# Down projection: five right-hand operands split during the gates and parked in DRAM, products reordered, ends on DVE

## The chip, the cores and the metric

One core of one Trainium2 chip runs the kernel. The metric is the device time of one execution in microseconds (us). Three executions before the change took 2123.8, 2124.66 and 2126.33; the median is 2124.66.

The engines that the text names: PE (matmul), ACT (ScalarE), DVE (VectorE), POOL (GpSimd), SP (the queue that issues most DMAs).

## The reference, cut to what matters

One block of a diffusion backbone on 1024 latent tokens with `D_MODEL` 1024, `D_FF` 2816, batch 1, all in float32, and a context prefix of 256 tokens. The two places of the change:

```python
merged = jax.nn.sigmoid(gate_a) * (y_a @ w_a) + jax.nn.sigmoid(gate_b) * (y_b @ w_b)
return merged @ w_o
...
a, v = jnp.split(h @ w_up, 2, axis=-1)
a = dwconv_grid(a, conv_w, conv_b) if on_grid else dwconv_seq(a, conv_w, conv_b)
return (jax.nn.gelu(a) * v) @ w_down
```

`w_down` is 2816 x 1024. The result of the block goes through a residual addition and a final RMSNorm to the output.

## The kernel before

**Products.** A float32 operand is split into a high part (rounded to fp32r, by an ACT cast) and a low part (the rest, by a subtraction). A product is three matmuls, high x high, high x low and low x high (`mm3`, L97 to L99). One matmul of 512 columns follows the one before in 0.23 us.

**Weights.** All weights come in units of 128 x 1024 elements (512 KB). A unit is loaded by SP into one of three slots `wraw` (`W_RAW`), cast by ACT into one of three slots `whi` and subtracted into one of three slots `wlo` (`W_SPL`), on POOL in the gates (L79). A slot is free again when its last reader is done: for `wraw` the subtraction, for `whi` and `wlo` the last matmul of the unit. Each engine and the queue of SP work strictly in the order that was written down at build time; an instruction that waits holds all behind it.

**Stages named here.** Gate A (about 967 to 1145 us): for each block m of 8, a unit of `w_in` (G0 to G7) and a unit of `w_branch_a` (B0 to B7), 48 matmuls each. Gate B (about 1145 to 1330): the same with `w_in` (G'0 to G'7) and `w_branch_b` (B'0 to B'7), in the order G'0, G'1, B'0, G'2, B'1 and so on; its inputs `ybl` and `ybh` are eight tiles that are loaded, cast and split at the border, when B7 has let go of the buffers. Beside both gates runs `mod_step`: a load `maw` of 512 KB into one buffer and a multiply-add on DVE. Then the output projection, the up projection with the convolution, and from 1871 us the down projection.

**Down projection.** It is done as Strassen's scheme with seven products on quarters (A: hidden values, B: `w_down`), each over six units `u` of two 128-row pieces (the last of one), 24 matmuls to a unit, 132 to a product. Four of the seven right-hand operands are differences of quarters of `w_down`; `sums_down(m)` makes them in gate A, for m below 6: four loads, four DVE subtractions (L113), four stores `t_d`. In the down projection every right-hand unit is loaded raw, cast by ACT (L1238) and subtracted by DVE (L1239). The left-hand operand of a unit is made by DVE (sums, L1213; low part, L1199) and ACT (cast, L1198). Behind the units stand the `ends`: additions of products out of PSUM (DVE), multiplication by the gate `g2b` and the residual addition (`gmul` L1316, `gadd` L1317, on POOL), the sum of squares (ACT), the factor of the norm, and the store. `reload(1)` loads the second half of the hidden values, 22 loads in one block behind the last weight load of the first product.

Of the kernel before, what the change touches and what calls it, by code (L numbers as in the profile page):

```python
# [8 lines left out]
F32 = mybir.dt.float32  # L9
# [26 lines left out]
def kernel(  # L36
# [29 lines left out]
    t_d = {(i, u): dram.tile([P, 1024], F32, name=f"t{i}_d{u}") for i in (1, 2, 3, 4) for u in range(NU)}  # L66
# [44 lines left out]
    def sums_down(u):  # L111
        n = unit_len(u) * 512
        sub = lambda o, a, b: nc.vector.tensor_tensor(out=o, in0=a, in1=b, op=ALU.subtract)  # L113
        keep = lambda i, t: nc.sync.dma_start(out=t_d[i, u][:, 0:n], in_=t)
        b12, b11 = raw_down(u, 0, 512), raw_down(u, 0, 0)
        sub(b11, b12, b11)
        keep(1, b11)
        b22 = raw_down(u, 1, 512)
        sub(b12, b22, b12)
        keep(3, b12)  # L120
        sub(b22, b22, b11)
        keep(2, b22)
        b21 = raw_down(u, 1, 0)
        sub(b21, b21, b22)
        keep(4, b21)
# [734 lines left out]

    for m in range(KC):
# [317 lines left out]
    reload(0)  # L1179
# [54 lines left out]
    def parts_b(raw, u):  # L1234
        n = unit_len(u) * 512
        hi = wp.tile([P, 1024], F32R, tag="whi", name="whi", bufs=W_SPL)[:, 0:n]
        lo = wp.tile([P, 1024], F32R, tag="wlo", name="wlo", bufs=W_SPL)[:, 0:n]
        nc.scalar.copy(out=hi, in_=raw)  # L1238
        nc.vector.tensor_tensor(out=lo, in0=raw, in1=f32(hi), op=ALU.subtract)  # L1239
        return v2(hi, u), v2(lo, u)  # L1240

    def quarter_b(half, c0):
        return lambda u: raw_down(u, half, c0)

    def summed_b(i):
        def f(u):
            n = unit_len(u) * 512
            raw = wp.tile([P, 1024], F32, tag="wraw", name="wraw", bufs=W_RAW)[:, 0:n]
            nc.sync.dma_start(out=raw, in_=t_d[i, u][:, 0:n])
            return raw  # L1250
        return f

    def product_d(acc, fa, fb, first, tail=0, done=None, post=()):
# [11 lines left out]
        for u in range(NU):  # L1265
            b = parts_b(fb(u), u)
# [27 lines left out]
    def half_row(n, cs, dst, junk):  # L1294

        nc.scalar.activation(out=junk, in_=dst, func=AF.Square, accum_out=sq0[:, n:n + 1])
        nc.gpsimd.tensor_tensor(out=dst, in0=dst, in1=fwb[:, cs], op=ALU.mult)
# [16 lines left out]
    W, X = banks("wy"), banks("xz")  # L1314
    u3 = p1
    gmul = lambda o, a, b: nc.gpsimd.tensor_tensor(out=o, in0=a, in1=b, op=ALU.mult)  # L1316
    gadd = lambda o, a, b: nc.gpsimd.tensor_tensor(out=o, in0=a, in1=b, op=ALU.add)  # L1317
    each = lambda f: [[lambda n=n: f(n)] for n in range(4)]

    def end_11(n):  # L1320
# [3 lines left out]
        half_row(n, lo_c, y, X[n])  # L1324
# [16 lines left out]
    def end_21a(n):  # L1341
        xl, v = stream(4 + n, lo_c), u3[:, n, :]
        nc.vector.tensor_add(out=v, in0=Z[n], in1=u2[:, n, :])
        gmul(v, v, g2b[:, lo_c])
        gadd(v, xl, v)

    def end_21b(n):
        rss[n] = row_sum(4 + n, u3[:, n, :], Z[n])

        xh = stream(n, hi_c)  # L1350
        gmul(u2[:, n, :], u2[:, n, :], g2b[:, hi_c])
        gadd(u2[:, n, :], xh, u2[:, n, :])

    def end_21c(n):
        row_end(4 + n, lo_c, u3[:, n, :], y3[1][:, n, :], hi_c, rss[n])
# [22 lines left out]
    product_d(Y, S4, quarter_b(1, 512), False, tail=3, done=end_12, post=[[lambda f=f, n=n: f(n) for f, n in g] for g in ends])  # L1378
# [39 lines left out]
```

## Time and profile before

| what | us |
|---|---|
| median of three runs | 2124.66 |
| the profiled execution | 2125.61 |
| its span | 2123.9 |
| PE busy in the span | 2048.9 (96%) |
| DVE, ACT, POOL busy | 1232.5, 781.5, 630.6 |
| gate A, gate B | 967 to 1145, 1145 to 1330 |
| down projection, first to last matmul | 1871 to 2115 |

The profile is one execution. A row of groups gives the busy time of a kind of instruction and the mean of one; a row of waits gives the time in which the engine named first stood still until the one named behind the arrow was done. Busy PE means that matmuls are in flight, so where the share is below the stretch's length PE had nothing to do. PEclk is the granted clock, 1.00 the level of 2.4 GHz and 0.50 that of 1.2 GHz.

### The profile page before, as it was taken

What the parts mean: (1) busy time and instruction counts of PE and PEld (TensorE: products, weight loads), DVE (VectorE), ACT (ScalarE), POOL (GpSimd) and SP (SyncE); (2) the same over time, 40 slices, a digit from 0 to 9 for tenths busy, and PEclk for the clock granted to TensorE, in tenths of its full rate; (3) what the DMA queues carried; (4) which work ended last, traced back from release to release, by engine and by line L of the source; (5) the groups of instructions that cost most, each with busy time, mean ns of one, the idle gap of its engine ahead of it and who ended that gap; (6) DMA issues with size and microseconds to landing.
All of it is one profiled execution on the core that took longest, in us unless ns stands there. A gap on an engine that the chain in (4) does not pass through costs nothing.

```text
span 2123.9 us, 27510 instructions
## 1 busy us (share of the span) xinstructions
PE 2048.9 (96%) x11138; PEld 1736.3 (82%) x11138; DVE 1232.5 (58%) x1695; ACT 781.5 (37%) x1103; POOL 630.6 (30%) x375
## 2 busy tenths in 40 slices
PE   7989999999999999999999999999999999989995
PEld 3879889889889899888787878997778888878873
DVE  4784364374374372445343234364798888878855
ACT  3765354255355341221112112234333333343432
POOL 2130212122122111211222220256666666401045
PEclk9989999999999999999999999999999999999997
DMA  7630111111111111116875332521232222385333
GB/s 268 208 90 21 42 49 32 49 41 42 39 40 60 31 47 54 50 50 220 265 218 169 109 102 82 189 76 31 70 100 80 74 85 89 98 306 192 118 122 121
DMA packets 206272, 219.30 MB, mean 103 GB/s; under 512 B 7795, under 2 KB 165816, under 8 KB 205121
## 3 DMA queue, kind: packets, MB, share of 16 engines
q1 hardware_dynamic: 204113, 212.57, 31.2%
q10 hardware_dynamic: 2032, 4.99, 0.6%
q8 instruction: 87, 1.43, 0.3%
q14 instruction: 40, 0.33, 0.1%
HBM read 178.97 MB, written 38.55 MB: 102 GB/s over the span
## 4 chain that ended last, share of the span: by engine, by line
PE 75%; DVE 10%; issue 6%; ACT 3%; DMA 3%; POOL 3%; SPq 0%; ACTq 0%; POOLq 0%; DVEq 0%
PE pj L99 13%; PE pj L97 13%; PE pj L98 13%; PE pq L97 5%; PE pq L99 5%; PE pq L98 5%; PE hg L97 3%; PE hg L99 3%; PE hg L98 3%; DVE acc L1152 2%; PE hg L691 1%; PE hg L673 1%; PE hg L710 1%; PE hg L797 1%; DVE b L354 1%
## 5 line engine op out<-in xcount | busy, mean ns | idle before, releaser
L79 POOL TENSOR_TENSOR wlo<-wraw,whi 128x1024 fp32r<-128x1024 f32 x88 | 221.0, 2515 | 706.1 <-ACT whi L78 687.3
L97 PE MATMUL pj<-hxh,whi 128*128 128x512 f32 x896 | 353.0, 394 | 0.2 <-ACT hxh L438 0.2
L98 PE MATMUL pj<-hxl,whi 128*128 128x512 f32 x896 | 351.1, 392 | 1.0 <-POOL hxl L439 1.0
L99 PE MATMUL pj<-hxh,wlo 128*128 128x512 f32 x896 | 351.1, 392 | 0.0
L78 ACT CAST whi<-wraw 128x1024 fp32r<-128x1024 f32 x124 | 129.3, 1049 | 380.8 <-PE pj L98 171.4
L1152 DVE SCALAR_TENSOR_TENSOR acc<-apad,cw,acc 128x1024 f32<-128x1024 f32 x176 | 226.3, 1286 | 20.8 <-ACT acc L1150 17.4
L97 PEld LDWEIGHTS pj<-hxh,whi 128*128 128x128 f32 x896 | 168.7, 188 | 35.3 <-issue 0.9
L98 PEld LDWEIGHTS pj<-hxl,whi 128*128 128x128 f32 x896 | 168.6, 188 | 34.3 <-POOL hxl L439 1.3
L99 PEld LDWEIGHTS pj<-hxh,wlo 128*128 128x128 f32 x896 | 168.6, 188 | 34.1
L97 PE MATMUL pj<-whi,hxh 128*128 128x256 f32 x512 | 145.5, 285 | 0.0
L99 PE MATMUL pj<-whi,hxl 128*128 128x256 f32 x512 | 145.3, 284 | 0.0
L98 PE MATMUL pj<-wlo,hxh 128*128 128x256 f32 x512 | 145.2, 284 | 0.0
L354 DVE TENSOR_TENSOR_SCAN b<-scanm,g 128x512 f32<-128x512 bf16 (+1 forms) x24 | 26.2, 1093 | 176.7 <-ACT g L601 174.7
L825 DVE SCALAR_TENSOR_TENSOR acc<-maw,sc,acc 128x1024 f32<-128x1024 f32 x32 | 49.7, 1554 | 98.2 <-DMA maw<-in_ada_w_dram 94.8
L98 PEld LDWEIGHTS pj<-wlo,hxh 128*128 128x128 f32 x512 | 98.4, 192 | 0.4 <-issue 0.2
L97 PEld LDWEIGHTS pj<-whi,hxh 128*128 128x128 f32 x512 | 98.2, 192 | 0.4 <-issue 0.2
L99 PEld LDWEIGHTS pj<-whi,hxl 128*128 128x128 f32 x512 | 98.5, 192 | 0.0
L156 POOL TENSOR_TENSOR rs<-ss,mhalf 128x4 f32<-128x4 f32 (+1 forms) x21 | 19.6, 934 | 262.1 <-DVE ss L720 210.9
L79 DVE TENSOR_TENSOR wlo<-wraw,whi 128x1024 fp32r<-128x1024 f32 x36 | 43.6, 1219 | 53.8 <-ACT whi L78 53.8
L97 PE MATMUL pj<-whi,mh 128*128 128x256 f32 x256 | 72.9, 285 | 0.0
L98 PE MATMUL pj<-wlo,mh 128*128 128x256 f32 x256 | 72.5, 283 | 0.0
L99 PE MATMUL pj<-whi,ml 128*128 128x256 f32 x256 | 72.4, 283 | 0.0
(451 smaller groups left out, 5131.8 us busy)
## 6 DMA issues: line engine op xcount, KB each, us to landing
wraw<-in_w_in_dram SPq DMA_DIRECT2D x96, 512.0 KB
wraw<-in_ffn_w_up_dram SPq DMA_DIRECT2D x44, 512.0 KB
wraw<-in_ffn_w_down_dram SPq DMA_DIRECT2D x35, 512.0 KB
maw<-in_ada_w_dram SPq DMA_DIRECT2D x32, 512.0 KB
hid_d<-hd SPq DMA_DIRECT2D x22, 512.0 KB
t_d<-wraw SPq DMA_DIRECT2D x20, 512.0 KB
wraw<-t_d SPq DMA_DIRECT2D x20, 512.0 KB
ring<-in_ada_w_dram SPq DMA_DIRECT2D x8, 1024.0 KB
```

Of the source, the lines that this page charges most:

```text
L78: nc.scalar.copy(out=hi, in_=raw)
L79: (lo_eng or nc.gpsimd).tensor_tensor(out=lo, in0=raw, in1=hi.bitcast(F32), op=ALU.subtract)
L97: nc.tensor.matmul(ps, lhsT=ah, rhs=bh, start=first, stop=False, **kw)
L98: nc.tensor.matmul(ps, lhsT=ah, rhs=bl, start=False, stop=False, **kw)
L99: nc.tensor.matmul(ps, lhsT=al, rhs=bh, start=False, stop=last, **kw)
L354: nc.vector.tensor_tensor_scan(out=b, data0=scanm[:, :n], data1=g, initial=0.0, op0=ALU.mult, op1=ALU.add)
L673: nc.tensor.matmul(quart(spv[:, i, d, :])[:, :, 1 - d, :], lhsT=e2[:, d, blk], rhs=quart(dm[:, d, blk])[:, :, 1 - d, :], start=True, stop= ...
L691: nc.tensor.matmul(kv[:, n * P:(n + 1) * P], lhsT=kt[:, n, :], rhs=vv[:, blks[n], :], start=True, stop=True)
L710: nc.tensor.matmul(o, lhsT=asum[:, n, :], rhs=vv[:, blk, :], start=True, stop=False)
L797: nc.tensor.matmul(mp[:, i * P:(i + 1) * P], lhsT=vt[4 * q + i][:, g_ * P:(g_ + 1) * P], rhs=wst[:, g_, :], start=True, stop=True)
L825: nc.vector.scalar_tensor_tensor(out=acc, in0=aw, scalar=sc[:, k, 0:1], in1=acc, op0=ALU.mult, op1=ALU.add)
L1152: nc.vector.scalar_tensor_tensor(out=grid(acc), in0=src, scalar=w_, in1=grid(acc), op0=ALU.mult, op1=ALU.add)
```

## The change

**In the gates.** `sums_down` becomes the generator `parts_down`. Its step makes one right-hand operand of one unit (`t1`, `b22`, `t3`, `t2`, `t4`) and splits it at once: the subtraction as before, then a cast on ACT into a `whi` slot, a low part on DVE into a `wlo` slot, and two stores, high and low, to `w_d`. There are 30 steps; `ahead_down(2)` runs two of them behind each block m, through gate A (16) and gate B (14). The raw quarters `b12`, `b11` and `b22` of a unit stay in their `wraw` slots over several steps. Against before, 30 casts, 30 low parts and 36 stores are added, and the work stretches over both gates.

**In the down projection.** For five products the parts are loaded from `w_d` into `whi` and `wlo` (`parts_b`), with no cast and no subtraction; the first two products split raw quarters as before (`split_b`). The order of the products becomes X A11, X A12, W S2, Y S1, Z S3, Y S4, Z A22, so that the last one has a plain quarter on the left, not a sum. All `gmul` and `gadd` work moves to DVE as plain operations (L1361, L1362, L1370, L1371, L1382, L1383). `reload(1)` is spread over the first seven units, three or four loads at a time.

```diff
+    def parts_down():
+        for u in range(NU):
+            n = unit_len(u) * 512
+            def keep(i, raw):
+                hi = wp.tile([P, 1024], F32R, tag="whi", name="whi", bufs=W_SPL)[:, 0:n]
+                lo = wp.tile([P, 1024], F32R, tag="wlo", name="wlo", bufs=W_SPL)[:, 0:n]
+                nc.scalar.copy(out=hi, in_=raw)
+                nc.vector.tensor_tensor(out=lo, in0=raw, in1=hi.bitcast(F32), op=ALU.subtract)
+                for t, d_ in zip((hi, lo), w_d[i, u]):
+                    nc.sync.dma_start(out=d_[:, 0:n], in_=t.bitcast(F32))
...
+            sub(b11, b12, b11)
+            keep("t1", b11)
+            yield
+            b22 = raw_down(u, 1, 512)
+            keep("b22", b22)
+            yield
+            sub(b12, b22, b12)
+            keep("t3", b12)
+            yield
...
-        if m < NU:
-            sums_down(m)
+        ahead_down(2)
...
         if prev is not None:
             fin_b(*prev)
+        ahead_down(2)
...
+    def parts_b(i):
         def f(u):
...
+            for x, d_ in zip(("whi", "wlo"), w_d[i, u]):
+                t = wp.tile([P, 1024], F32R, tag=x, name=x, bufs=W_SPL)[:, 0:n]
+                last_load[0] = nc.sync.dma_start(out=t.bitcast(F32), in_=d_[:, 0:n])
...
+    def end_12a(n):
+        xl, v = stream(n, hi_c), u3[:, n, :]
+        nc.vector.tensor_add(out=v, in0=Y[n], in1=u2[:, n, :])
+        nc.vector.tensor_mul(out=v, in0=v, in1=g2b[:, hi_c])
+        nc.vector.tensor_add(out=v, in0=xl, in1=v)
...
-    product_d(X, A11, quarter_b(0, 0), True)
-    with tc.issue_after(ins_of(last_load[0])):
-        reload(1)
...
-    product_d(Z, S3, summed_b(3), True, post=each(end_w))
-    product_d(Y, S1, summed_b(1), True, post=each(end_z))
-    product_d(Z, A22, summed_b(4), False, post=each(end_22))
-    product_d(Y, S4, quarter_b(1, 512), False, tail=3, done=end_12, ...
+    product_d(X, A11, split_b(0, 0), True, post=[rows(3)] * 5)
...
+    product_d(X, A12, split_b(1, 0), False, post=[rows(4)] * 2)
+    product_d(W, S2, parts_b("t2"), True, post=run(end_11a))
+    product_d(Y, S1, parts_b("t1"), True, post=run(end_w, end_11b))
+    product_d(Z, S3, parts_b("t3"), True, post=run(end_y))
+    product_d(Y, S4, parts_b("b22"), False, post=run(end_22))
+    product_d(Z, A22, parts_b("t4"), False, tail=3, done=end_21, ...
```

The lines of the kernel after are 1 to 40 higher than those before. The order of the instructions is made by a scheduler when the kernel is built, so three places are shown as it stands there.

SP's queue at the border of the gates, before. `wraw` from `w_in` and `w_branch_b` are weight units, here G'1, B'0, G'2 and B'1; `ybl` are the loads at the border.

```order
L85 DMA wraw_9287<-in_w_in_dram 128x8x128
L85 DMA wraw_9348<-in_w_branch_b_dram 128x8x128
L85 DMA wraw_9412<-in_w_in_dram 128x8x128
L85 DMA wraw_9473<-in_w_branch_b_dram 128x8x128
L875 DMA ybl0_9189<-yb_d0_63 128x1024
L875 DMA ybl1_9190<-yb_d1_64 128x1024
```

The same place after, from the load of G'0 (9299) on; 9379 is G'1 and 9440 B'0.

```order
L86 DMA wraw_9299<-in_w_in_dram 128x8x128
L123 DMA t1h_d3_101<-whi_9252 128x1024
L123 DMA t1l_d3_102<-wlo_9253 128x1024
L107 DMA wraw_9363<-in_ffn_w_down_dram 128x2x512
L123 DMA b22h_d3_89<-whi_9365 128x1024
L897 DMA ybl0_9266<-yb_d0_63 128x1024
```

```order
L838 DMA acc_9357<-in_ada_b_dram 1x1024
L841 DMA maw_9360<-in_ada_w_dram 128x1024
L123 DMA b22l_d3_90<-wlo_9366 128x1024
L123 DMA t3h_d3_125<-whi_9372 128x1024
L123 DMA t3l_d3_126<-wlo_9373 128x1024
L86 DMA wraw_9379<-in_w_in_dram 128x8x128
L841 DMA maw_9437<-in_ada_w_dram 128x1024
L86 DMA wraw_9440<-in_w_branch_b_dram 128x8x128
```

The next weight units stood ahead of the border's loads; now one stands ahead, and G'1 behind all of them and behind the store of a low part that DVE has yet to make. Between the two pieces stand the other `ybl` loads.

SP's queue in blocks 3 and 4 of gate A after; 8541 and 8602 are G3 and B3, 8687 is G4, 8671 the raw `b22` of unit 1.

```order
L86 DMA wraw_8541<-in_w_in_dram 128x8x128
L123 DMA t1l_d1_98<-wlo_8535 128x1024
L86 DMA wraw_8602<-in_w_branch_a_dram 128x8x128
L107 DMA wraw_8671<-in_ffn_w_down_dram 128x2x512
L123 DMA b22h_d1_85<-whi_8673 128x1024
L123 DMA b22l_d1_86<-wlo_8674 128x1024
L86 DMA wraw_8687<-in_w_in_dram 128x8x128
L123 DMA t3h_d1_121<-whi_8680 128x1024
L123 DMA t3l_d1_122<-wlo_8681 128x1024
L86 DMA wraw_8751<-in_w_branch_a_dram 128x8x128
```

Before, no store here waited for a cast, and the four stores of a unit were of the raw slots themselves.

POOL's end of the program before (its last product's work; `p` and `u` are rows of the result), of which after only the `ss` lines are left:

```order
L1316 TENSOR_TENSOR p_14799<-p_14799,g2b 128x512
L1316 TENSOR_TENSOR u_14800<-u_14800,g2b 128x512
L1317 TENSOR_TENSOR p_14799<-xl,p_14799 128x512
L1317 TENSOR_TENSOR u_14800<-xl,u_14800 128x512
L1316 TENSOR_TENSOR p_14799<-p_14799,g2b 128x512
L1316 TENSOR_TENSOR u_14800<-u_14800,g2b 128x512
L1317 TENSOR_TENSOR p_14799<-xl,p_14799 128x512
```

DVE's last product after, where this work now stands between the low parts of the left operand (L1224):

```order
L1369 TENSOR_TENSOR p_14991<-xy,u_14992 128x512
L1224 TENSOR_TENSOR b21l<-b22h,b21h 128x1024
L1370 TENSOR_TENSOR p_14991<-p_14991,g2b 128x512
L1369 TENSOR_TENSOR p_14991<-xy,u_14992 128x512 x2
L1370 TENSOR_TENSOR p_14991<-p_14991,g2b 128x512 x2
L1371 TENSOR_TENSOR p_14991<-xl,p_14991 128x512
L1369 TENSOR_TENSOR p_14991<-xy,u_14992 128x512
L1371 TENSOR_TENSOR p_14991<-xl,p_14991 128x512
L1370 TENSOR_TENSOR p_14991<-p_14991,g2b 128x512
L1330 TENSOR_TENSOR ss_16286<-ss_16286,sq_14999 128x1
L1224 TENSOR_TENSOR b21l<-b22l,b21h 128x1024
```

Ten operations of the ends stand on DVE ahead of the low part of unit 3; the subtractions of the right operand (L1239 before) are gone from there.

## Rows read from the trace of the kernel before

**Rows 1.** Windows view: stretch, us, busy us per engine, PEclk, DMA share, GB/s.

```profile
967.00:1145.00 178.00, 178.00 (x790) 146.02 (x788) 71.15 (x62) 29.22 (x36) 38.28 (x16) 1.00 0.70 223
1145.00:1330.00 185.00, 185.00 (x821) 149.56 (x821) 73.92 (x77) 41.48 (x48) 35.45 (x14) 1.00 0.37 116
1871.00:1900.00 29.00, 26.70 (x110) 21.41 (x109) 22.93 (x21) 9.06 (x10) 0.00 (x0) 0.94 0.98 331
1900.00:1910.00 10.00, 8.02 (x34) 6.04 (x33) 3.61 (x4) 4.96 (x8) 0.00 (x0) 1.00 0.77 287
2050.00:2060.00 10.00, 8.20 (x36) 6.49 (x36) 3.69 (x4) 4.17 (x5) 1.23 (x1) 1.00 0.64 209
2100.00:2105.00 5.00, 3.42 (x7) 2.44 (x8) 2.08 (x3) 1.06 (x2) 0.00 (x0) 0.50 0.57 210
```

**Rows 2.** PE's timeline, start of the last product: start us, us, operation.

```profile
2060.22 0.39 PE L99 MATMUL xz<-whi,b21l 128*128 128x512 f32 x1
2060.45 0.39 PE L97 MATMUL wy<-whi,b11h 128*128 128x512 f32 x1
```

**Rows 3.** PE's timeline after the late wait, and the last matmul.

```profile
2102.90 0.63 PE L99 MATMUL wy<-whi,b11l 128*128 128x512 f32 x1
2103.33 0.63 PE L97 MATMUL wy<-whi,b21h 128*128 128x512 f32 x1
...
2114.47 0.39 PE L99 MATMUL wy<-whi,b11l 128*128 128x512 f32 x1
```

**Rows 4.** Waits, 2060 to 2124 us: total us, times, longest us.

```profile
PE wy L98 <- DVE wlo L1239: 11.3, 3, 7.3
...
POOL p L1316 <- DVE p L1343: 15.9, 1, 15.9
```

**Rows 5.** Groups by line, POOL, 2020 to 2100 us: busy us, mean ns.

```profile
L1316 POOL TENSOR_TENSOR u<-u,g2b 128x512 f32<-128x512 f32 x4 | 8.2, 2038 | 0.0
```

**Rows 6.** The same for DVE, 2020 to 2124 us.

```profile
L1239 DVE TENSOR_TENSOR wlo<-wraw,whi 128x1024 fp32r<-128x1024 f32 (+1 forms) x12 | 18.5, 1545 | 6.5 <-ACT whi L1238 6.5
...
L1334 DVE TENSOR_TENSOR y<-wy,p 128x512 f32<-128x512 f32 x4 | 2.7, 682 | 2.9 <-PE wy L99 2.9
```

**Rows 7.** The chain of waits: start us, us, what.

```profile
1888.56 3.65 DMA hid_d<-hd
```

**Rows 8.** SP's timeline in the first gate: a weight load's issue.

```profile
996.70 0.46 SPq L85 DMA_DIRECT2D wraw<-in_w_in_dram  x1
```

**Rows 9.** ACT's timeline beside it: the cast that waits for that load.

```profile
1002.81 1.05 ACT L78 CAST whi<-wraw 128x1024 fp32r<-128x1024 f32 x1 [5.87 <-DMA wraw<-in_w_in_dram]
```

**Rows 10.** SP's timeline at the border of the gates and behind it.

```profile
1126.86 0.37 SPq L85 DMA_DIRECT2D wraw<-in_w_in_dram  x1
...
1140.26 3.04 SPq L875 DMA_DIRECT2D ybl<-yb_d  x5
...
1178.80 5.94 SPq L824 DMA_DIRECT2D maw<-in_ada_w_dram  x2
```

**Rows 11.** ACT's timeline at the border.

```profile
1143.54 1.05 ACT L876 CAST ybh<-ybl 128x1024 fp32r<-128x1024 f32 x1 [7.81 <-DMA ybl<-yb_d]
...
1146.07 1.04 ACT L876 CAST ybh<-ybl 128x1024 fp32r<-128x1024 f32 x1
1147.32 1.05 ACT L876 CAST ybh<-ybl 128x1024 fp32r<-128x1024 f32 x1 [0.21 <-DMA ybl<-yb_d]
```

**Rows 12.** DVE's timeline at the border.

```profile
1145.77 0.68 DVE L866 TENSOR_TENSOR mg<-hg,sg 128x512 f32<-128x512 f32 x1
```

**Rows 13.** Groups by line, DVE, 967 to 1145 us.

```profile
L825 DVE SCALAR_TENSOR_TENSOR acc<-maw,sc,acc 128x1024 f32<-128x1024 f32 x16 | 27.2, 1698 | 45.4 <-DMA maw<-in_ada_w_dram 42.0 <-DMA acc<-in_ada_b_dram 3.3
L113 DVE TENSOR_TENSOR wraw<-wraw 128x1024 f32<-128x1024 f32 (+1 forms) x21 | 25.6, 1220 | 38.1 <-DMA wraw<-in_ffn_w_down_dram 34.4 <-issue 3.3
...
L820 DVE MEMSET acc<- 128x1024 f32 x2 | 1.8, 912 | 0.4 <-DVE yal L785 0.3 <-issue 0.2
```

**Rows 14.** The same for POOL.

```profile
L79 POOL TENSOR_TENSOR wlo<-wraw,whi 128x1024 fp32r<-128x1024 f32 x16 | 38.3, 2393 | 141.5 <-ACT whi L78 141.5
```

More of the change, by code (lines that the diff above doesn't have):

```diff
@@ L65 @@
     NU = (NJ // 2 + 1) // 2
-    t_d = {(i, u): dram.tile([P, 1024], F32, name=f"t{i}_d{u}") for i in (1, 2, 3, 4) for u in range(NU)}
+    B_NAMES = ("b22", "t1", "t2", "t3", "t4")
+    w_d = {(i, u): [dram.tile([P, 1024], F32, name=f"{i}{x}_d{u}") for x in "hl"] for i in B_NAMES for u in range(NU)}
     s2_d = [dram.tile([P, 1024], F32, name=f"s2_d{u}") for u in range(NU)]
@@ L109, in raw_down @@
         return raw
[L111 to L125, printed above, removed]
+    def parts_down():
[8 more added lines that the diff above has]
+                    nc.sync.dma_start(out=d_[:, 0:n], in_=t.bitcast(F32))
+            sub = lambda o, a, b: nc.vector.tensor_tensor(out=o, in0=a, in1=b, op=ALU.subtract)
+            b12, b11 = raw_down(u, 0, 512), raw_down(u, 0, 0)
+            sub(b11, b12, b11)
[7 more added lines that the diff above has]
+            yield
+            sub(b22, b22, b11)
+            keep("t2", b22)
+            yield
+            b21 = raw_down(u, 1, 0)
+            sub(b21, b21, b22)
+            keep("t4", b21)
+            yield
     ident = const.tile([P, P], F32, name="ident")
@@ L859, in branch, with ahead_down @@
         mod_step()
+    down_steps = parts_down()
+    def ahead_down(n):
+        for _ in range(n):
+            next(down_steps, None)
     for m in range(KC):
@@ L1177, in reload @@
                     nc.sync.dma_start(out=H[f][u][:, i, sl], in_=hid_d[f * HK + 2 * u + i][:, sl])
-    reload(0)
+                    yield
+    for _ in reload(0):
+        pass
     dn, close_dn = pool("dn", "right")
@@ L1296, in half_row @@
         nc.scalar.activation(out=junk, in_=dst, func=AF.Square, accum_out=sq0[:, n:n + 1])
-        nc.gpsimd.tensor_tensor(out=dst, in0=dst, in1=fwb[:, cs], op=ALU.mult)
+        nc.vector.tensor_mul(out=dst, in0=dst, in1=fwb[:, cs])
     def row_sum(n, val, junk):
@@ L1312, in row_end, with end_11a @@
         nc.sync.dma_start(out=out[0, n * P:(n + 1) * P, cs], in_=val)
-    W, X = banks("wy"), banks("xz")
+    W, X = banks("wz"), banks("xy")
     u3 = p1
[L1316 to L1320, printed above, removed]
+    def end_11a(n):
         xl, y = stream(n, lo_c), y3[0][:, n, :]
@@ L1337, in end_22 @@
         half_row(4 + n, hi_c, y, xl)
     rss = {}
[L1341 to L1355, printed above, removed]
@@ L1370, with run, rows, f @@
+    def run(*fs):
+        return [[lambda f=f, n=n: f(n) for f in fs] for n in range(4)]
+    more = reload(1)
+    def rows(n):
+        def f():
+            with tc.issue_after(ins_of(last_load[0])):
+                for _ in range(n):
+                    next(more, None)
+        return [f]
+    product_d(X, A11, split_b(0, 0), True, post=[rows(3)] * 5)
     for n in range(4):
         nc.scalar.copy(out=p1[:, n, :], in_=X[n])
-    product_d(X, A12, quarter_b(1, 0), False)
-    product_d(W, S2, summed_b(2), True, post=each(end_11))
@@ L1374 @@
-    Y, Z = banks("wy"), banks("xz")
-    product_d(Z, S3, summed_b(3), True, post=each(end_w))
-    product_d(Y, S1, summed_b(1), True, post=each(end_z))
-    product_d(Z, A22, summed_b(4), False, post=each(end_22))
-    product_d(Y, S4, quarter_b(1, 512), False, tail=3, done=end_12, post=[[lambda f=f, n=n: f(n) for f, n in g] for g in ends])
+    product_d(X, A12, split_b(1, 0), False, post=[rows(4)] * 2)
+    product_d(W, S2, parts_b("t2"), True, post=run(end_11a))
+    Y, Z = banks("xy"), banks("wz")
@@ L1379 @@
+    product_d(Y, S1, parts_b("t1"), True, post=run(end_w, end_11b))
+    product_d(Z, S3, parts_b("t3"), True, post=run(end_y))
+    product_d(Y, S4, parts_b("b22"), False, post=run(end_22))
+    product_d(Z, A22, parts_b("t4"), False, tail=3, done=end_21,
+              post=[[lambda f=f, n=n: f(n) for f, n in g] for g in ends])
     close_dn()
```

61 lines of the change are left out of this document (35 added, 26 removed).

## The prediction

> **What bounds the kernel now.** I read the windows view first: which engine has no idle time, stage by stage. In both gates PE is busy for the whole stretch, 178.00 of 178 us and 185.00 of 185 [rows 1]. So there the matmuls set the time, all else is cover, and any weight that comes late is paid in full. DMA is not idle cover: 223 GB/s in gate A, 116 in gate B. In the down projection the picture differs: PE lacks 2.3 us between 1871 and 1900, 2.0 in the next 10 us and 1.8 between 2050 and 2060 [rows 1]. Then PE's timeline: the last product starts at 2060.45, its matmuls stand 0.23 apart [rows 2], and 132 of them (0.227 each) would end at 2090.4. The last one starts at 2114.47 and lasts 0.39 [rows 3], so it ends at 2114.86: the last product loses 24.4 us. The waits say to what: PE to the low part of the right-hand operand on DVE, 11.3 us in three waits, longest 7.3 [rows 4]. DVE is late because its queue holds operations that wait for POOL's ends: POOL waited 15.9 us for the first of them [rows 4], and then each took about 2 us, 2038 ns mean in the group of `u` [rows 5]. Low parts on DVE average 1545 ns there [rows 6], against 1220 for the same shape in gate A [rows 13]. After the waits the matmuls run 0.43 apart [rows 3] at a granted clock of 0.50 [rows 1], the 1.2 GHz level, which is inside the 24.4.
>
> So the change touches one stage with 24 us to win and one in which everything has to stay hidden.
>
> **The down projection.** *Last product.* Gone from DVE: six subtractions of the right operand; gone from POOL: all its large operations. DVE now has six low parts (five of 1.22, one of 0.68) and for each of four rows five operations of 0.68 [rows 6] and one of about that size, some 17 us: 24 us of work in 30. Ahead of the low part of unit 3 stand ten of them; with two low parts that is 10 x 0.68 + 2 x 1.22 = 9.2 us from the product's start, and unit 3 is due at 16.4. Unit 4 arrives at about 15, due at 18. The tightest is the load of unit 4's parts: in SP's queue it stands behind two stores that wait for DVE's row ends at about 13, and it lands around 20. I take 3 us of stall in place of 24.4: **gain 21.4**. Taken at worst, DVE in order ends 10 us late; at best nothing is late.
>
> *Start.* With `reload(1)` spread, the weight loads no longer queue behind 22 loads; half of the 4.3 us lost before 1910 goes: **gain 2.1**, between 0 and 4.3. *2050 to 2060*: POOL's ends of the sixth product go, 1.0 of the 1.8. The part loads double the bytes of a right-hand unit (1 MB in the 5.45 us of 24 matmuls, 192 GB/s); the three-slot rings let a unit's load start two units (10.9 us) ahead, and the stage ran at 331 GB/s [rows 1], so I cost this at nothing; without the lookahead it would cost about 5 us. The tail behind the last matmul has the same operations with new names: nothing. Sum 24.5; bounds 14 and 29.
>
> **The gates, the price.** The 30 casts (1.05 [rows 9]) and 30 low parts (1.22, the row of the same shape [rows 13]) lie on engines that idle there: nothing by themselves. What costs is what they hold. A raw slot is kept over steps, so that weight units go one after another through what is left; a split slot is free again only when its store has landed; and SP holds a weight load behind stores that wait for DVE and ACT. So I followed this chain by hand with these durations: store to landing 3.65 [rows 7]; cast 1.05; DVE 1.22, `mg` 0.68, `acc` 1.70 [rows 6, 13]; POOL's low part 2.39 [rows 14]; issue 0.4 [rows 8]. For a load there are two ends: 6.1 in gate A, issued at 996.70 and cast from 1002.81 [rows 8, 9]; and 4.2 in gate B, where two `maw` issues through one buffer take 5.94 [rows 10], less the second issue (0.33) and the multiply-add (1.28 when undisturbed, and 0.1 of hand-over). In the new chain loads go one at a time, as in the second row, but weight units are strided, as in the first: 4.6, nearer to the lower.
>
> *G3 and G4* (0 is the start of G2; a gate unit of 48 matmuls takes 10.9). I take the raw `b11` of unit 1 as issued at 3.5, from the same reckoning one block earlier; it lands at 8.1. Subtraction, `mg`, `acc`, low part: 12.9. Cast and store of t1: 14.4. G3's load is issued at 14.8, lands at 19.4, cast and low part end at 22.8; its third matmul wants that at 22.25: 0.6 late. B3's load waits for that slot: low part at 31.3, in time. Raw `b22` behind it lands at 36.3, its low part is done at 39.4, the store lands at 43.5, t3's low part takes that slot (44.7), its store lands at 48.7, and G4's low part takes the slot after it: 51.1, wanted at 45.1. **6.6 late in both.** At 4.2 per load it is 4.4, at 6.1 about 12.6.
>
> *The border.* B7 ends at 1145.8, where `mg` follows [rows 12]; call that E. Before, G'1 was on its way by 1126.86 and the `ybl` loads began at 1140.26 [rows 10]. Now SP reaches them only when G'0's low part has freed a slot (E - 4.9 by the same chain), raw `b22` has come (E + 0.1) and been cast: first `ybl` at E + 1.9. ACT must first cast t3 (ready E + 6.2, when a store has landed); five `ybh` casts at 1.25 apart [rows 11] end at E + 12.3, DVE's subtraction at 13.5, the `acc` memset (0.91 [rows 13]) at 14.4, t3's low part at 15.6. Behind its store SP issues G'1 at E + 16.4: landed 21.0, low part 24.4. PE has G'0 until E + 11.4 and wants the low part at 11.8. **12.6 late**, 11.0 at 4.2 per load, 18.6 at 6.1. Behind G'1 stand a multiply-add, B'0 and G'2; B'0 is 10.9 later on PE and arrives in time.
>
> *Others*: G6 1.0 (0 to 3); unit 4 in gate B 2.0 (0 to 5). *Clock*: after the border PE restarts at half rate as after 2100, when 3.4 us of matmuls at 0.50 lost half [rows 1]; with a trace of it at G4: 2.4. Sum 6.6 + 12.6 + 1.0 + 2.0 + 2.4 = 24.6; bounds 18 and 43 (the rivals below).
>
> The trace puts 0.94 on 1871 to 1900, where the stalls were short [rows 1]. The Trainium skill, "TensorE: Matmul & The Clock Gate" (Part 1), says that the default state is throttled and activity releases the throttle. By that G4's stall of 6 us would be followed by a half-rate stretch as long as the border's, some 1.5 us more; the sum here goes by the rows.
>
> **Sum.** 2125.61 + 24.6 - 24.5 = 2125.7 against the profiled execution, which stands 0.95 above the median: **2124.8**. A measurement of this kernel tells about 0.2% (4.2 us) from no change.
>
> **Rivals.**
>
> *Loads are quicker: faster.* With every load at the 4.2 of gate B, the gates cost 4.4 + 11.0 + 0 + 1.0 + 2.0 = 18.4, and with the down projection near its best (28) the time is 2115. For it: each load now has few others beside it. Against it: the store landings stay. The page "DMA: Bandwidth & Descriptors" of the Trainium skill (Anatomy of one DMA) fits a DMA as 2.0 us plus bytes over 436 GB/s, for another queue than SP's; that gives an estimate of 3.2 us for 512 KB, with which four loads in each of the two chains would end 5.6 earlier than at 4.6, and this rival at 2107. No row here is so short: 4.2 is the least. Chance 0.28.
>
> *The border and G4 by slow landings: slower.* One mechanism: the chain through the slots runs at gate A's 6.1 per load, since two stores now go with each step. Then 12.6 + 18.6 + 3 + 5 + 3.5 = 42.7, and 2143. It decides from about 5.0 per load, each 0.1 being worth 1 us over the ten loads that lie on these chains. For it: gate B's traffic doubles (14 steps of 1.4 MB on 116 GB/s); against it: gate A keeps its mean. Chance 0.22.
>
> *DVE becomes the bound of the last product: slower.* If its 24 us of work, in order, leave unit 5 ten us late, the gain is 17.5 and the time 2132. For it: 24 of 30 us is a tight fit in order. Against it: the hand chain has unit 5 in time. Chance 0.05.
>
> That the change does not do what it says I leave out: the order on the engines shows the casts gone from the last five products.
>
> **How the numbers follow.** My forecast, 0.45, has its own range of 2115 to 2134 (each sum off by some 7), nearly even around no change: 0.14 faster, 0.17 same, 0.14 slower. With the quick case all faster (0.28), the slow ones slower (0.27, of which I count 0.01 as same): faster 0.42, same 0.18, slower 0.40. The range leaves out one in ten on each side: 2107 to 2142.
>
> **What would show it.** In the profile after: PE idle of about 12 us right behind G'0 with G'1's cast as the wait, and `ybl` loads some 7 us later against B7's end; idle of about 6 before G4; low clock behind both; the last product at about 33 us for 132 matmuls, no large POOL operation in it. I am wrong if the gates stay full (then about 2100), or if the last product still waits for DVE by more than 10.

## The result and the profile after

| | median of runs, us | lowest to highest | ratio to before, 95% interval |
|---|---|---|---|
| before | 2124.23 (4 runs) | 2122.23 to 2126.33 | |
| after | 2139.02 (4 runs) | 2135.28 to 2141.89 | 1.0068 (1.0050 to 1.0087) |

The change makes the kernel 0.7% slower, more than the 0.2% that can be told from no change. The forecast was 2124.8, no change; the result lies 14.2 above it, within the range (2107 to 2142), and 4 us below the rival with the slow landings (2143).

The profiled execution took 2139.41, 13.8 more than the one of before. PE's timeline splits that at the first and the last matmul of the down projection (before 1871.58 and 2114.47): 38.8 are lost between gate A's start and the down projection, 26.4 are won in it, 1.0 is lost in the tail behind the last matmul, and 0.4 ahead of the gates. Both large terms were forecast, at 24.6 and 24.5.

The windows view of after, the columns as in [rows 1]; first both gates, then the three stalls of gate A, then the border:

```profile
967.00:1145.00 178.00, 170.34 (x723) 137.55 (x722) 71.99 (x62) 39.41 (x46) 33.34 (x14) 0.96 0.60 201
1145.00:1330.00 185.00, 162.29 (x693) 130.27 (x693) 86.15 (x82) 46.26 (x55) 32.08 (x13) 0.94 0.65 213
...
1030.00:1040.00 10.00, 7.50 (x29) 5.49 (x28) 3.11 (x3) 1.54 (x2) 2.35 (x1) 0.92 0.56 178
1060.00:1070.00 10.00, 7.27 (x20) 4.04 (x19) 0.00 (x0) 3.54 (x4) 4.72 (x2) 0.78 0.51 165
1110.00:1120.00 10.00, 7.57 (x26) 5.49 (x25) 3.99 (x2) 1.52 (x2) 2.35 (x1) 0.84 0.49 160
1170.00:1180.00 10.00, 3.80 (x17) 2.82 (x15) 6.42 (x8) 6.30 (x7) 0.00 (x0) 0.92 0.88 304
1180.00:1190.00 10.00, 0.00 (x0) 0.00 (x0) 8.17 (x8) 4.10 (x5) 0.00 (x0) 0.50 0.92 318
1190.00:1200.00 10.00, 3.50 (x7) 2.33 (x8) 4.44 (x2) 3.04 (x3) 4.34 (x2) 0.50 0.66 195
```

Where [rows 1] showed PE busy for all of 178 and 185 us, it is now idle for 7.7 and 22.7, and behind each stall the granted clock is below 1.00. Between 1180 and 1190 PE does nothing at all.

PE's timeline of after at the border (start us, us, operation, idle before and what ended it):

```profile
1173.41 0.39 PE L100 MATMUL pj<-hxh,wlo 128*128 128x512 f32 x1
1195.24 0.79 PE L98 MATMUL pj<-hxh,whi 128*128 128x512 f32 x1 [21.44 <-ACT whi L79]
1195.83 0.63 PE L99 MATMUL pj<-hxl,whi 128*128 128x512 f32 x1
1197.72 0.80 PE L100 MATMUL pj<-hxh,wlo 128*128 128x512 f32 x1 [1.26 <-POOL wlo L80]
```

The stall stands right behind G'0, with G'1's cast as the wait, as forecast, but it is 21.4 + 1.3 us long and not 12.6.

For a measure of each step I take the four marks that the gates carry anyway: the block of four small matmuls `hg<-acc,ones` (L830 before, L847 after), one in every 16 units. In before they stand at 1056.1, 1145.2, 1234.3 and 1323.4, 89.1 apart; the first quarter counts from the block `hg<-wst,vt` at 967.1. G3 lies in the first quarter, G4 and G6 in the second, the border in the third, unit 4 and the rest of gate B in the fourth. What each quarter is longer than in before, in us:

| kernel | 1st | 2nd | 3rd | 4th | gates |
|---|---|---|---|---|---|
| forecast | 0.6 | 7.0 | 15.0 (12.6 and the clock, 2.4) | 2.0 | 24.6 |
| after | 4.7 | 10.5 | 25.9 | 0.3 | 41.4 |
| border's steps one block later | 2.3 | 11.4 | 12.5 | 5.9 | 32.1 |
| high stores on ACT's queue | 7.1 | 7.2 | 21.5 | 2.2 | 38.0 |
| no stores | -0.1 | 0.0 | 8.8 | 0.0 | 8.7 |
| parking alone (e3) | 3.7 | 10.4 | 23.1 | 1.1 | 38.3 |
| ends on POOL (e4) | 1.3 | 9.5 | 25.9 | 0.7 | 37.4 |

(The last five are experiments, below.) In the gates e3 and e4 run the same instructions as after, in the same order on every engine and queue. So one execution of these gates costs 37.4 to 41.4, and a difference of 4 between two kernels is not one that these profiles can tell. Of after's 41.4, 2.6 come back before the down projection, at one place: PE's wait for a low part on POOL (`qlo`) is 4.46 us long in before, up to 1506.79, and 2.77 in after, up to 1547.18, and the matmuls right behind it stand closer.

In the last product, after, by the windows view:

```profile
2094.72:2127.26 32.54, 30.48 (x132) 24.36 (x131) 23.03 (x45) 10.26 (x20) 5.02 (x6) 1.00 0.77 270
```

and PE's waits in it (total us, times, longest us):

```profile
PE wz L99 <- DMA wlo<-t4l_d: 1.3, 1, 1.3
PE wz L98 <- DMA whi<-t4h_d: 0.7, 1, 0.7
```

Beside the 11.3 us for DVE's low part in [rows 4] there are 2.0 now, for the parts' load, and the clock is 1.00.

### The profile page after: what moved, and what is told of

Same layout as the page of the kernel before. It is cut to its first block, busy times and chain, and to the rows that moved or that the text cites. A ratio compares the mean times of both kernels' runs of the same rounds, so it can differ in the third digit from the quotient of the medians.

```text
span 2137.7 us, 27662 instructions
## 1 busy us (share of the span) xinstructions
PE 2053.3 (96%) x11138; PEld 1739.9 (81%) x11138; DVE 1245.9 (58%) x1727; ACT 783.4 (37%) x1103; POOL 579.1 (27%) x343
## 5 line engine op out<-in xcount | busy, mean ns | idle before, releaser
L1175 DVE SCALAR_TENSOR_TENSOR acc<-apad,cw,acc 128x1024 f32<-128x1024 f32 x176 | 226.3, 1286 | 21.1 <-ACT acc L1173 17.7
L842 DVE SCALAR_TENSOR_TENSOR acc<-maw,sc,acc 128x1024 f32<-128x1024 f32 x32 | 56.2, 1755 | 86.0 <-DMA maw<-in_ada_w_dram 83.1
L120 ACT CAST whi<-wraw 128x1024 fp32r<-128x1024 f32 (+1 forms) x30 | 29.4, 979 | 144.6 <-DVE wraw L125 30.3
L173 POOL TENSOR_TENSOR ss<-ss,mhalf 128x1 f32<-128x1 f32 x16 | 11.4, 717 | 245.8 <-DVE ss L1330 213.6
L125 DVE TENSOR_TENSOR wraw<-wraw 128x1024 f32<-128x1024 f32 (+1 forms) x24 | 27.5, 1148 | 81.1 <-DMA wraw<-in_ffn_w_down_dram 80.8
```

The costliest lines, as they stand in the source:

```text
L173: nc.gpsimd.tensor_tensor(out=dst, in0=src, in1=mhalf[:, :n], op=ALU.pow)
L842: nc.vector.scalar_tensor_tensor(out=acc, in0=aw, scalar=sc[:, k, 0:1], in1=acc, op0=ALU.mult, op1=ALU.add)
L1175: nc.vector.scalar_tensor_tensor(out=grid(acc), in0=src, scalar=w_, in1=grid(acc), op0=ALU.mult, op1=ALU.add)
```

## The experiments

The same table for the down projection, from PE's timeline of each kernel: from its first matmul to the last product's first, and from there to the last matmul's start. 132 matmuls at 0.227 take 29.7.

| kernel | right operands | order | ends | `reload(1)` | six products | last product | sum |
|---|---|---|---|---|---|---|---|
| before | split there | old | POOL | block | 188.9 | 54.0 | 242.9 |
| after | parked | new | DVE | spread | 183.9 | 32.5 | 216.5 |
| e2 | split there | new | DVE | spread | 184.4 | 31.9 | 216.3 |
| e3 | parked | old | POOL | block | 186.4 | 39.6 | 226.0 |
| e4 | parked | new | POOL | spread | 184.1 | 40.1 | 224.2 |
| e5 | split there | new | POOL | spread | 186.2 | 45.4 | 231.6 |
| e6 | split there | old | DVE | block | 187.1 | 30.8 | 218.0 |
| e7 | split there | new | DVE | block | 188.2 | 31.9 | 220.0 |
| e9 | split there | old | DVE | spread | 183.9 | 30.0 | 213.9 |

**Border's steps one block later (e1).** Gate B's first block makes no steps, so that SP's queue has only the stores of gate A's last step ahead of G'1's load, and no step beside the `ybl` loads.

```diff
-        ahead_down(2)
+        ahead_down(2 if m else 0)
```

> One edit to the changed kernel: block 0 of gate B runs no step of the parts, so all steps of gate B move one block later (blocks 1 to 7 instead of 0 to 6). G'1's load then stands in SP's queue ahead of the border's ybl loads. Theory 'queue order': the 22 us of idle PE at the border come from G'1's load standing behind the ybl loads and t3's low store; then nearly all of it and its slow clock go: about 24 us less than the changed kernel, 2115, and the three smaller stalls in gate A stay as they are. Rival 'traffic': the bytes themselves are too many there (ybl, two stores a step, raw loads), and the wait only moves to the next units: at most 6 us less, 2133.

Measured: 2127.79, ratio 1.0011 (1.0001 to 1.0022). PE's waits in both gates (total us, times, longest us):

```profile
PE pj L100 <- POOL wlo L80: 8.9, 5, 1.9
PE pj L98 <- ACT whi L79: 5.9, 4, 2.0
PE hg L100 <- POOL wlo L80: 1.7, 1, 1.7
PE hg L98 <- ACT whi L79: 1.4, 1, 1.4
```

The time lies between the two expectations (2115 and 2133). The long wait is gone: no wait is above 2.0, where after had one of 21.4. In after G'1's load was issued 11.7 us after PE had run out of work (1173.80 to 1185.52), so most of that stall was made by the order on SP's queue at the border; e1 also takes the load and the stores of two steps away from there, and doesn't tell order and traffic apart. The quarters return only 9 of the 41: the third still loses 12.5, with four short waits, and the fourth 5.9. The steps are dear wherever they stand.

**No parking, all else of the change (e2).** `sums_down` goes back into gate A; in the down projection all seven right operands are loaded raw and split there.

```diff
-            for x, d_ in zip(("whi", "wlo"), w_d[i, u]):
-                t = wp.tile([P, 1024], F32R, tag=x, name=x, bufs=W_SPL)[:, 0:n]
-                last_load[0] = nc.sync.dma_start(out=t.bitcast(F32), in_=d_[:, 0:n])
...
+            raw = wp.tile([P, 1024], F32, tag="wraw", name="wraw", bufs=W_RAW)[:, 0:n]
+            last_load[0] = nc.sync.dma_start(out=raw, in_=t_d[int(i[1]), u][:, 0:n])
+            return split_raw(raw, u)
```

> Only the down projection of the change: gates as before (four sums, raw stores, gate A only), right-hand operands loaded raw and split by ACT and DVE in every product as before, but the new order of products, the ends on DVE and the spread reload. Theory 'order and ends': what shortened the down projection by 26 us is that the last product has a plain left operand and no POOL ends; it keeps at least 20 of the 26, and the gates lose nothing: about 2104 or less. Rival 'parked parts': DVE needs to be rid of the 30 subtractions; with 6 x 1.22 us more in the last product it has 31 us of work in a product of 30 and loses 10 or more there: 2112 or more.

Measured: 2097.1, ratio 0.9868 (0.9851 to 0.9884), 1.3% faster than before. The way to the down projection takes 901.5 us (901.5 to 904.4 in the six kernels with the gates of before), and the down projection 216.3, as long as with the parked parts. Parking is paid with 34 to 39 us ahead of the down projection (38.8 in after, 37.0 in e3, 34.1 in e4) and gives nothing in it, as long as the ends are on DVE.

**Parking alone (e3).** Gates and part loads of after; product order, ends on POOL and `reload(1)` in a block as before.

> Only the parking of the change: gates as in the changed kernel, parts loaded in the down projection, but the old order of products (the sum S4 last), the ends on POOL and reload in one block. Theory 'order and ends': the last product still waits for POOL's 27 us of ends and loses most of its 24 us, so about 2155. Rival 'parked parts': DVE without its subtractions is in time although POOL is slow, so the last product loses under 10: about 2143.

Measured: 2146.37, ratio 1.0095 (1.0080 to 1.0110). The down projection is 16.9 shorter than before; 37.0 are lost ahead of it. The last product is 9.9 above the 29.7, as in the second expectation: while the ends are on POOL, parking does help.

**Parking and the new order, ends on POOL (e4).** One of the three pairs of lines that change; the multiplication in `half_row` goes to POOL too.

```diff
-        nc.vector.tensor_mul(out=v, in0=v, in1=g2b[:, hi_c])
-        nc.vector.tensor_add(out=v, in0=xl, in1=v)
+        nc.gpsimd.tensor_tensor(out=v, in0=v, in1=g2b[:, hi_c], op=ALU.mult)
+        nc.gpsimd.tensor_tensor(out=v, in0=xl, in1=v, op=ALU.add)
```

> The changed kernel with the multiplications by the gate, residual additions and weight multiplications of the ends back on POOL, nothing else. Theory 'ends on DVE matter': 20 POOL operations of 1.3 to 2 us in the last product are 26 to 40 us in 30, the row ends come late and DVE's low parts behind them too: 6 to 12 us slower than the changed kernel. Rival 'POOL hides': with the parts loaded, DVE has room to wait: within 2 us of the changed kernel.

Measured: 2144.67, ratio 1.0090 (1.0075 to 1.0105). The last product takes 40.1, 7.6 more than in after. The waits of its last stage show how POOL reaches PE (total us, times, longest us):

```profile
ACT xy L1329 <- POOL p L1371: 12.6, 3, 11.1
...
PE wz L98 <- DMA whi<-t4h_d: 7.4, 2, 6.5
```

PE doesn't wait for POOL. It waits for a part load (issued at 2109.04), which stands in SP's queue behind two stores of results (2104.95), and these wait through ACT's sum of squares for POOL's additions.

**The new order alone, ends on POOL (e5).** The edit of e4 on e2.

> The kernel of e2 (gates as before, nothing parked, new order of products, spread reload) with the ends on POOL instead of DVE. If the order of the products alone makes the gain (a plain left operand in the last product, so DVE is late by less): down projection within 3 us of e2's 216.3 from first to last matmul, time about 2099. If the ends on DVE are needed: POOL's chain in the last product comes late as in e4 (7.9 us there) and DVE has its subtractions besides: 8 to 16 us more than e2, 2106 to 2113.

Measured: 2112.97, ratio 0.9946 (0.9932 to 0.9961). The last product takes 45.4; from its waits:

```profile
PE wz L98 <- DVE wlo L1241: 12.3, 2, 9.5
...
DVE p L1322 <- POOL ss L156: 8.0, 3, 6.5
```

It is the wait of [rows 4], 12.3 for 11.3: DVE's subtraction, in order behind operations that wait for POOL's. The second line is one of these waits, for `ss`, the factor of the norm.

**The ends on DVE alone (e6).** The kernel before, with `half_row` and these two lines changed.

```diff
-    gmul = lambda o, a, b: nc.gpsimd.tensor_tensor(out=o, in0=a, in1=b, op=ALU.mult)
-    gadd = lambda o, a, b: nc.gpsimd.tensor_tensor(out=o, in0=a, in1=b, op=ALU.add)
+    gmul = lambda o, a, b: nc.vector.tensor_tensor(out=o, in0=a, in1=b, op=ALU.mult)
+    gadd = lambda o, a, b: nc.vector.tensor_tensor(out=o, in0=a, in1=b, op=ALU.add)
```

> The kernel before with one edit: all large operations of the ends on DVE instead of POOL; old order of products, nothing parked, reload in one block. If POOL's slow chain in front of DVE's in-order subtractions is what costs the last product its 24 us: at least 15 of them come back, 2109 or less. If the order matters (sums and subtractions of S4 and of the quarter on DVE, 12 x 1.2 us and more, beside some 17 us of ends): DVE has over 30 us of work in the last product and at most 8 come back, 2116 or more.

Measured: 2096.89, ratio 0.9872 (0.9857 to 0.9887). The last product takes 30.8 for 54.0. The windows view of it, before and then e6:

```profile
2060.45:2114.70 54.25, 36.23 (x133) 26.94 (x131) 33.79 (x45) 17.24 (x29) 29.90 (x22) 0.78 0.38 133
```

```profile
2052.40:2083.50 31.10, 30.35 (x133) 24.44 (x131) 30.59 (x55) 13.89 (x25) 7.33 (x6) 1.00 0.44 153
```

and DVE's groups with the shapes kept apart (busy us, mean ns, idle before), first before, 2020 to 2124 us, then e6, 2052 to 2093:

```profile
L1239 DVE TENSOR_TENSOR wlo<-wraw,whi 128x1024 fp32r<-128x1024 f32 x10 | 17.2, 1716 | 4.9 <-ACT whi L1238 4.9
```

```profile
L1239 DVE TENSOR_TENSOR wlo<-wraw,whi 128x1024 fp32r<-128x1024 f32 x4 | 4.9, 1218 | 0.0
...
L1316 DVE TENSOR_TENSOR u<-u,g2b 128x512 f32<-128x512 f32 x4 | 2.7, 686 | 0.0
```

The multiplication that took POOL 2038 ns [rows 5] takes DVE 686, and the subtractions of 128x1024 fall from 1716 to 1218. (The 1545 of [rows 6] is a mean over two shapes.) DVE is busy for 30.59 of 31.10 us with all subtractions still on it, and PE loses 0.8 us in one wait, for ACT. So these lines alone win the last product.

**The price of the block reload (e7).** e2 with `reload(1)` in one block behind the first product.

```diff
-    product_d(X, A11, split_b(0, 0), True, post=[rows(3)] * 5)
+    product_d(X, A11, split_b(0, 0), True)
+    with tc.issue_after(ins_of(last_load[0])):
+        for _ in more:
+            pass
```

> The kernel of e2 with the 22 loads of the second half of the hidden values in one block behind the first product's last weight load, as before. If the spread helped, the stalls behind the first product come back: about 2 us more than e2 (2099), within what a measurement can tell; if the stalls there come from the splits of the first two products alone: no difference.

Measured: 2102.32, ratio 0.9896 (0.9877 to 0.9915). The six products take 188.2 for 184.4, so the spread is worth 3.7 in the trace; the medians differ by 5.2, and their intervals overlap.

**High stores on ACT's queue (e8).** After, with SP relieved of 30 of the 60 stores.

```diff
-                for t, d_ in zip((hi, lo), w_d[i, u]):
-                    nc.sync.dma_start(out=d_[:, 0:n], in_=t.bitcast(F32))
+                for e, t, d_ in zip((nc.scalar, nc.sync), (hi, lo), w_d[i, u]):
+                    e.dma_start(out=d_[:, 0:n], in_=t.bitcast(F32))
```

> The changed kernel with the stores of the high parts issued from ACT's queue behind the cast that makes them; the low parts stay on SP. Bytes, slots and landings are the same. If SP's order is what makes the weight units of gate A late (G3, G4, G6): their stalls shrink by half or more, the gates' 39 us become under 30. If it is the slots that wait for landed stores and for loads one after another: the three stalls stay within 1 us each, the time within 5 us of the changed kernel's.

Measured: 2135.21, ratio 1.0052 (1.0035 to 1.0069), 4 us below after, with overlapping intervals. PE's waits in both gates:

```profile
PE pj L98 <- ACT whi L79: 19.7, 3, 15.8
PE pj L100 <- POOL wlo L80: 8.3, 6, 1.8
```

The gates lose 38.0, within the 37.4 to 41.4 that the unchanged gates lose. The border's stall shrinks to 15.8, from 21.4 in after, 18.8 in e3 and 21.1 in e4. The others don't follow either expectation: G3's idle time grows from 2.5 to 4.2, G4's falls from 2.7 to 0.5, G6's goes from 2.4 to 3.0. So no clear gain shows from taking half of the stores out of SP's queue; that their bytes are on the way, and hold their slots, is not changed by this edit, nor is the low stores' wait for DVE on SP's queue. The last product, whose instructions and their order are those of after, takes 36.9 for 32.5: PE waits 3.8 for unit 4's parts instead of 2.0, and runs at half rate behind it.

**The best of both (e9).** e6 with `reload(1)` spread.

```diff
-    product_d(X, A11, quarter_b(0, 0), True)
-    with tc.issue_after(ins_of(last_load[0])):
-        reload(1)
+    product_d(X, A11, quarter_b(0, 0), True, post=[rows(3)] * 5)
...
-    product_d(X, A12, quarter_b(1, 0), False)
+    product_d(X, A12, quarter_b(1, 0), False, post=[rows(4)] * 2)
```

> The kernel of e6 (before with the ends on DVE) with the spread reload of the change. If the spread is worth what e7 lost against e2, the down projection shortens by 2 to 4 us from e6's 218: about 2094, the fastest of all. If e7's loss was that of the first split units and not of the block: within 1 us of e6, 2097.

Measured: 2094.99, ratio 0.9860 (0.9846 to 0.9875), the fastest kernel here. The windows view of its last product:

```profile
2051.00:2082.37 31.37, 31.37 (x138) 25.58 (x138) 30.86 (x55) 14.32 (x25) 7.34 (x6) 1.00 0.45 155
```

PE has no idle time left in it. Against e6 the six products take 183.9 for 187.1 and the last one 30.0 for 30.8; the medians differ by 1.9, and their intervals overlap. Against e2, which has the new order of the products, it is 2.4 shorter in the down projection, and e6 2.0 shorter than e7: with the ends on DVE the new order gains nothing either.

**No stores in the gates (e10).** This kernel leaves out what the down projection needs, so its time as a whole says nothing; the gates are compared.

```diff
-                for t, d_ in zip((hi, lo), w_d[i, u]):
-                    nc.sync.dma_start(out=d_[:, 0:n], in_=t.bitcast(F32))
...
+        return split_b(1, 512)
```

> The changed kernel with the 60 stores of the parts left out; the raw slots are held, the casts, subtractions and loads of the steps are there as in the changed kernel. The down projection takes a plain quarter of w_down, split there, in place of the five parked operands, so only the gates compare (from the mark at the start of gate A to the first matmul of the down projection: 904.5 before, 943.3 in the changed kernel). If split slots that wait for landed stores, and SP's queue behind them, make the gates late: the gates lose under 10 of the 39 us. If the held raw slots (weight units one after another) make them late: 25 or more stay.

Measured: 2105.18, ratio 0.9909 (0.9892 to 0.9925). All 30 steps run, with their loads, raw slots, casts and subtractions, and gate A is full again; the third quarter loses 8.8 in one place. This is the first expectation, under 10. The windows view of the gates:

```profile
967.00:1145.00 178.00, 178.00 (x777) 144.36 (x776) 77.19 (x70) 43.52 (x50) 36.81 (x15) 1.00 0.42 130
1145.00:1330.00 185.00, 179.26 (x772) 145.15 (x771) 89.35 (x93) 52.24 (x61) 38.52 (x15) 0.98 0.46 145
```

So the held raw slots, the longer work of ACT and DVE and the loads cost at most 8.7; some 33 of the 41.4 come with the stores. One thing moves along: without them the scheduler puts G'1's load ahead of the `ybl` loads, so a part of the 33 is the order at the border and not the stores' own time. e1 has G'1 ahead as well, with all its stores, and loses 32.1: so some 23 of the 33 come with the stores even where the order at the border is right, give or take the 4 by which such gates differ.

## Where the forecast was right and where it was wrong, step by step

**Right: the down projection.** The last product gained 21.5 (forecast 21.4), with 2.0 of waits for the very load that was named as the tightest, unit 4's. That the two sizes agree to 0.1 is partly luck: the same last product takes 33.5 in e1 and 36.9 in e8 for the 32.5 here, by longer waits for the parts. The other six gained 4.9, forecast 2.1 + 1.0 = 3.1; the start was undersized, since e7 puts the spread of `reload(1)` at 3.7 by itself (3.2 by e9 against e6). The loads of the parts cost next to nothing, as forecast: 216.5 with them, 216.3 without. The tail, forecast at nothing, took 1.0.

**Wrong in its reason: what frees DVE.** The step said "Gone from DVE: six subtractions of the right operand; gone from POOL: all its large operations", and took both as one gain. e6 has the second without the first and gains 23.2 in that product, more than the change. e3 and e4, which have the first without the second, gain 14.4 and 13.9. The two cures overlap, and parking is the one that isn't needed. With the subtractions on DVE it is busy for 98% of the product and PE hardly notices; the rival "DVE becomes the bound" had its price from the same mistrust of a full engine.

**Wrong in size: the gates.** The places were all named: G3, G4, G6 and the border stall, in this order, and the wait at the border is for G'1's cast. The sum was 24.6 and is 41.4. Of the 16.8 that it lacks, PE's idle time at the border makes 10.1 (22.7 for 12.6) and the clock 6.1 (8.5 for 2.4, below). G3 and G4 together stood idle for 5.2 (forecast 6.6) and G6 for 2.4 (1.0), unit 4's 2.0 in gate B did not come, and 2.5 are in none of these places. Three durations behind the sum were wrong: the load's, the store's landing and that of the low clock.

*The load at 4.6.* "4.6, nearer to the lower." No load that ACT waited for in these gates lies there; they fall into two groups. SP's timeline of after has the issues of G3 and G'1:

```profile
1028.30 0.46 SPq L86 DMA_DIRECT2D wraw<-in_w_in_dram  x1
...
1185.52 1.37 SPq L86 DMA_DIRECT2D wraw<-in_w_in_dram  x1
```

and ACT's timeline the casts of G3, G4 and G'1, where the bracket says how long ACT stood idle before and for what:

```profile
1034.43 1.05 ACT L79 CAST whi<-wraw 128x1024 fp32r<-128x1024 f32 x1 [6.04 <-DMA wraw<-in_w_in_dram]
...
1062.64 1.04 ACT L79 CAST whi<-wraw 128x1024 fp32r<-128x1024 f32 x1 [6.29 <-DMA t3h_d<-whi]
...
1194.14 1.04 ACT L79 CAST whi<-wraw 128x1024 fp32r<-128x1024 f32 x1 [8.38 <-DMA wraw<-in_w_in_dram]
```

From issue to cast G3 took 6.1 and G'1 8.6. Of the 17 weight loads of the gates for which ACT stood waiting, the 11 with a store issued within 4 us ahead of them or while they were on the way took 5.0 to 8.6; of the six without, four took 3.6 to 3.8, one 5.8, and one, 3.9 behind G'1's load, 7.5. Without any store (e10), 11 of 17 took 3.6 to 3.9 and none over 6.0; some of the longer ones there have another load close by. The trace of before had it already: eleven loads beside stores took 4.5 to 6.7, the 6.1 of [rows 8, 9] among them, and one without, issued at 1097.71 and cast from 1101.60, took 3.9, less than the 4.2 that the prediction calls the least. The rival with the slow landings gave this reason, "since two stores now go with each step". G3's load and G'1's, on the chains that matter, stand next to stores.

*The landing of a store at 3.65.* G4's cast waited not for its load but for a slot that the store of t3's high part held. That store was issued at 1055.88 and let go by 1062.64, 6.8 us later; at the border t1's was issued at 1152.75, and G'0's cast behind it began at 1158.72. DVE's group of the low parts shows the same in sum (idle before and its releasers, last columns):

```profile
L121 DVE TENSOR_TENSOR wlo<-wraw,whi 128x1024 fp32r<-128x1024 f32 (+1 forms) x30 | 37.2, 1239 | 28.5 <-DMA t3l_d<-wlo 8.2 <-ACT whi L120 6.7 <-DMA t4l_d<-wlo 6.5
```

The operation is about as short as forecast, 1239 ns (a mean over two shapes), but DVE stood idle ahead of them for 28.5 us, more than half of it (8.2 + 6.5) for stores.

*The border.* With E set by the mark (1160.78 + 0.6 as in before, so 1161.4), the chain runs against the forecast like this: G'0's low part ends at E + 1.2 (forecast E - 4.9); the first `ybl` issue stands at 1167.77, E + 6.4 (E + 1.9); G'1's load is issued at 1185.52, E + 24.1 (E + 16.4); its cast starts at E + 32.7 and the low part, begun at 1195.32, ends 2.35 later at 1197.67, E + 36.3 (E + 24.4). So the chain came to the border 6 late from the block before, SP let go of G'1 another 1.6 later, and the load took 4.0 more than the 4.6, behind eight `ybl` loads, a `maw` and three stores with the DMA engines at 0.92 [the window of 1180 to 1190 above].

*The clock.* 2.4 were put down for it, almost all at the border. PE's timeline shows matmuls some 0.43 apart behind every stall: for 3.4 us behind G3's, 5.7 behind G4's, 3.3 behind G6's, and 5.7 (without the second wait) at the border. At 0.43 for 0.227 each of these loses 47%: 8.5 in all. The Trainium skill, "TensorE: Matmul & The Clock Gate" (Part 1), says that activity releases the throttle; the prediction drew from it a half-rate stretch at G4 as long as the border's. The trace of after agrees, 5.7 and 5.7, and PE's idle time at G4 was only 0.7 and 2.0. But in e3 and e4, with the same instructions, half rate lasted about 3 us behind G4 and 5.6 and 6.1 at the border, so the two are not equal in general.

**The rivals.** Quick loads (2115) fell with the first windows. By the page "DMA: Bandwidth & Descriptors" of the Trainium skill (Anatomy of one DMA) a load would be an estimated 3.2, by a fit for another queue than SP's; no weight load of the gates that ACT waited for was under 3.59 from issue to cast, even with no store beside it (e10). The slow landings gave 2143 and were nearest, by the right mechanism: 42.7 in the gates (measured 41.4, of which 2.6 come back) against 24.5 in the down projection (26.4). That its sum comes so close is partly luck: it has G3, G4 and G6 at 15.6, and PE stood idle for 7.6 there; it has unit 4 at 5, and the last quarter lost 0.3; and it has 18.6 for the border's 22.7 and 3.5 for the clock's 8.5.

**Not settled.** How the 33 us divide between the time of the stores, the slots that they hold and the order that the scheduler makes because of them. e1 against e10 puts some 23 on the stores with G'1 ahead at the border; e8's 38.0 shows no share for the issues of half of the stores on SP, within 4 us. A version with slots of its own for the steps was not run.

## What to carry to other kernels

Where two parts of a change cure the same wait, price each alone: three lines that moved elementwise work from POOL to DVE gave 1.3%, and the 30 steps that were to relieve DVE cost 34 to 39 us and, beside those lines, gave nothing. Work that is put "under" a stage in which PE is full is priced by the slots and queue places that it takes, not by the engines' busy time; and a load's duration must be read from a row with the same neighbours that it will have. The 4.6 put between two clearly different durations was a value that none of the 17 loads had. And one profile of a stage with stalls is one draw: before a difference between two kernels is read as an effect, look at what two executions of the same instructions differ by.

## What the runs showed of the hardware

- A 512 KB weight load of the same shape on the same queue took, from issue to cast, 3.6 to 3.9 us in most cases with no store beside it (four of six in after, 11 of 17 in e10), and beside stores 5.0 to 8.6 in after and 4.5 to 6.7 in before. The issues of DMA in gate A of e10, without stores (KB each, median us to landing):

```profile
wraw<-in_w_in_dram SPq DMA_DIRECT2D x9, 512.0 KB, 3.5
wraw<-in_w_branch_a_dram SPq DMA_DIRECT2D x7, 512.0 KB, 3.6
```

- Two idle times of PE of 0.7 and 2.0 us, with 0.7 us of work between them, were followed by half rate (0.43 between matmuls) for 5.7 us; in e3 and e4 the same place gave about 3 us. Single idle times of 1.0, 1.75 and 1.4 us in e4 (up to 1035.92, 1111.00 and 1134.49) were followed by full rate, one of 1.75 in e3 (up to 1035.48) by half rate. From after:

```profile
1063.74 0.50 PE L98 MATMUL pj<-hxh,whi 128*128 128x512 f32 x1 [0.71 <-ACT whi L79]
...
1066.49 0.80 PE L100 MATMUL pj<-hxh,wlo 128*128 128x512 f32 x1 [2.02 <-POOL wlo L80]
1067.09 0.63 PE L98 MATMUL pj<-hxh,whi 128*128 128x512 f32 x1
1067.51 0.63 PE L99 MATMUL pj<-hxl,whi 128*128 128x512 f32 x1
```

- A multiplication of 128x512 took POOL 2038 ns while DVE worked beside it, and DVE 686; and DVE's own subtractions of 128x1024 fell from 1716 to 1218 ns when POOL's operations were gone. In before's last product the two that had POOL busy beside them from start to end (at 2070.4 and 2086.0) took 2.3 us each.
- An engine at 98% (DVE, 30.59 of 31.10 us, in order) cost PE one wait of 0.8 us, and that one ended with a cast on ACT.
